# Four up blocks begun product by product in a hybrid RWKV-7 / attention decoder block, with two sums in a PSUM bank and attention heads scaled a tile later

## The chip, the cores and the metric

The kernel runs on one core of a Trainium2 chip. The metric is the device time of one execution in microseconds (us); lower is better. A run gives the time of each execution, and one profiled execution gives a trace of every instruction and DMA.

The engines are TensorE (PE, matmuls and transposes; PEld is its weight load), VectorE (DVE), ScalarE (ACT), GpSimd (POOL) and SyncE (SP). DMAs are issued from the queues of SP, ACT and POOL, and each queue issues in order: a DMA that must wait holds what stands behind it. PSUM has eight banks of 2 KB per partition, each 512 float32 columns.

## The reference

One decoder layer on 512 tokens, width 2048, float32: RWKV-7 time mixing and sliding-window attention in parallel, merged by sigmoid gates, then a gated FFN with a causal convolution of width 3 over the tokens.

```python
def reference(x, ...):
    h = rms_norm(x, norm1_g)
    z = h @ w_in                       # 2048 -> 9152 columns
    o_rw = rwkv7_mix(token_shift(z[:, :RW_SHIFT_COLS], rw_mu), ...)   # 16 heads of 64
    o_att = swa_attention(q, k, v, q_norm_g, k_norm_g, sinks)         # q and k: rms_norm by head of 64
    g_rw, g_att = sigmoid(zg[:, :2048]), sigmoid(zg[:, 2048:])
    x = x + (g_rw * (o_rw @ w_branch[:1024]) + g_att * (o_att @ w_branch[1024:])) @ w_out
    return x + conv_ffn(rms_norm(x, norm2_g), w_up, conv_w, conv_b, w_down)

def conv_ffn(h, w_up, conv_w, conv_b, w_down):
    u = h @ w_up                       # 2048 -> 2 * 5632
    c = conv_w[0] * u[t - 2] + conv_w[1] * u[t - 1] + conv_w[2] * u[t] + conv_b
    val, gate = split(c, 2)
    return (silu(gate) * val) @ w_down # 5632 -> 2048
```

## The kernel before, in words

Tokens are the free dimension of nearly all tiles (512 columns), features the partitions (128). Every large matmul is done in three: both factors are split into a high part (rounded to float32r by ACT, `whi`) and a low part (the rest, a subtraction on DVE, `wlo`), and hi x hi, hi x lo and lo x hi are summed in PSUM.

A planner orders the instructions of each engine by its own estimate of when they are ready; `pin` keeps an instruction behind all that was traced before it on its engine. Semaphores follow the data, and the tiles' buffers. All weight loads stand in SP's queue.

**Attention and RWKV (about 35 to 1230 us).** `ztile` computes one 128-column tile of z (48 matmuls, four weight loads of 256 KB through four `raw` buffers). A k or q tile goes through `qk_norm`: DVE multiplies by the gain (zq), ACT squares (sqq), PE sums by head (`head_stats`), DVE takes the inverse root in some 12 small instructions (rq), PE transposes it, DVE copies it (rsT), and `head_rows` writes it to DRAM (rsd) and reads it back spread over 64 partitions per head (rsb): three DMAs from ACT's queue, the last two waiting for the first to land. Then DVE multiplies z by rsb. The k tile is copied into kd by four more DMAs from ACT. `head_rows` also serves each of the eight RWKV pairs twice, in `early` and `final`. `sums_along` puts sums of quarters of w_out and w_down into DRAM at every third (later 16th) weight load.

**Branch products (about 1210 to 1445 us).** o_rw and o_att times w_branch, scaled by the gates, which are read back from DRAM (gin, two DMAs per tile from ACT).

**w_out and w_down** are each multiplied in seven half-size products (Winograd's form of Strassen's scheme) over halves of the tokens and of the columns; `taken_out` adds a finished product into x1 (L917). The last product of w_out reads x by then normalised by `normalise(0)` for its token half 0; `transposed` turns x1 into `q11` and `q21` (token half 0) and `q12` and `q22` (half 1), and `split_q` splits them into hi and lo.

**Up blocks (about 1628 to 2550 us).** 44 blocks f of 128 value and 128 gate columns of w_up, each with seven products P1, P2, P7, P6, P5, Q4, P3, of 24 matmuls of 256 columns, hi and lo parts made two products ahead (`prep(i + 2)`) through three buffers. P1 and P2 need only b11 and b21 (token half 0); P7, P5, P6 and Q4 need t3, t1, t2 and t4, and P3 needs b22: differences of all four quarters. Three PSUM sums: X takes P1, P6, P5, P3 one on top of the other and is read after each; Z takes P2; Y takes P7 and Q4. `out` brings them to u:

```python
            if n == "P7": return
            if n in ("P1", "P6"): ... act.activation(t, X, AF.Copy)        # t1, u2  (L1031)
            if n == "P2":   dve: u[:, 0, first half] = Z + t1               # L1035
            elif n == "P5": act: u4 = X; dve: u[:, 1, second half] = Y + u4 # L1038, L1039
            elif n == "Q4": dve: u[:, 1, first half] = Y + u2               # L1041
            else:           act: u[:, 0, second half] = X                   # P3, L1043
```

X and Z are each half a bank of a tile with two buffers of its own (four banks), Y has two. `conv` does the convolution in five to seven pieces, one per `prep`; `keep` stores the factors of a pair of blocks to DRAM, from ACT's queue, before the first piece of every second block. The order of the products is written out in `steps`; matmuls, splits and `out` are pinned. Two blocks are begun together; from block 2 the order is P7, P6, P2, P5, P1 of the next block, Q4, P3. Loads are issued in the order of `queue`, each group when a named earlier product has been prepared. a11 has two buffers; a12, s3, s1 and a22 share six; s3 and s1 are sums of two quarters, the second added by a DMA from POOL.

Of the kernel before, what the change touches and what calls it, by code (L numbers as in the profile page):

```python
# [134 lines left out]
def block_kernel(ctx: ExitStack, tc: tile.TileContext, d: Dims, a: dict, out: bass.AP):  # L135
# [147 lines left out]
    if True:  # L283
# [63 lines left out]

        with ExitStack() as pt:
# [7 lines left out]
            def qk_norm(acc, gain, dst):  # L356
                z = ap_.tile([P, S], F32, name="zq", tag="zq", bufs=2)
# [6 lines left out]
                rb = head_rows(ap_, small(), rs)  # L364
                dve.tensor_tensor(dst, z, rb, op=ALU.mult)
# [4 lines left out]
            for t in range(NKV):  # L370
                acc = ztile(d.c_ka + t * P)
                kn = ap_.tile([P, S], F32, name="kn", tag="kn", bufs=2)
                qk_norm(acc, col("kg"), kn)
                for h in range(2):
                    for e in range(2):
                        act.dma_start(kd[2 * t + h][e * HD : (e + 1) * HD], kn[h * HD : (h + 1) * HD])
                acc = ztile(d.c_va + t * P)
                vf = ap_.tile([P, S], F32, name="vf", tag="zq", bufs=2)
# [18 lines left out]
            for g in range(NHK):  # L397
# [3 lines left out]
                else:  # L401
                    emit_gate()
                oT = ap_.tile([P, GQ // 2, S], F32, name="oT", tag="oT", bufs=2)
# [358 lines left out]
        with tc.tile_pool(name="ain", bufs=1, side="right", reuse_waits="tile") as ainp:  # L762
# [24 lines left out]
    x1 = x1p.tile([P, NT, d.D], F32, name="x1")  # L787
# [29 lines left out]
    wp["step"] = 16  # L817
    with ExitStack() as pbb:
# [9 lines left out]
        for m, i in order:  # L828
            hi, lo, r0, n, gi = parts[i]
            second = m in g  # L830
            if not second:
                g[m] = tb.tile([P, 2, S], F32, name="gin", tag="gin")
                for j in range(2):
                    act.dma_start(g[m][:, j], gate_d[(j * NK + m) * P : (j * NK + m + 1) * P])
            acc = accp.tile([P, S], F32, name="acc", tag="acc")
            project(acc, a["w_b"][m].rearrange("p (k c) -> p k c", c=P)[:, r0 : r0 + n], hi, lo)
            if second:
                w = min(XC, d.D)
                for e in range(m * XC, (m + 1) * XC, w):
                    t, c0 = divmod(e, d.D)  # L840
                    with tc.issue_after(wp["last"].ins):
                        sync.dma_start(x1[:, t, c0 : c0 + w], xd[t * P : (t + 1) * P, c0 : c0 + w])
# [63 lines left out]
    def taken_out(i, acc, xr, scale, done):  # L906
        ci, tj, sign = PRODUCTS[i][4]
        last = i in (3, 4, 5, 6)
        for t in range(NT // 2):
            for e in range(NQW):  # L910
                tt = tj * NT // 2 + t
                cs = slice(ci * DH + e * S, ci * DH + (e + 1) * S)
                x = xr[:, tt, cs]
# [13 lines left out]
    q11, q12, q21, q22 = (x1[:, 2 * j : 2 * j + 2, i * WC : (i + 1) * WC] for i in range(2) for j in range(2))  # L927
    tpx = ExitStack()

    def row_done(i, t, cc, cs):  # L930
        sq = sqp.tile([P, S], F32, name="sqc", tag="sqc", bufs=2)
        act.activation(sq, x1[:, t, cs], AF.Square, accum_out=ssp[:, t, cc : cc + 1])
        (act if i == 6 else pool).dma_start(x1_d[t * P : (t + 1) * P, cs], x1[:, t, cs])

    def normalise(h):
# [3 lines left out]
        for i in range(2):  # L939
            for t in range(NT // 2):  # L940
                part = x1[:, 2 * h + t, i * WC : (i + 1) * WC]
# [5 lines left out]
    def transposed(tps, i, h, q):  # L947

        pss = []
        for k in range(KH):  # L950
            if k % 2 == 0:
                pss.append(tps.tile([P, 2, TH], F32, name="ps_t", tag="tp"))
            for t in range(NT // 2):
                pe.transpose(pss[-1][:, k % 2, t * P : (t + 1) * P],
                             x1[:, 2 * h + t, (i * KH + k) * P : (i * KH + k + 1) * P], ident)
# [19 lines left out]
    def half(nm, n=1):  # L975
        return up.tile([P, TH], F32, name=nm, tag=nm, bufs=n)

    class Block:
# [6 lines left out]
        def load(self, *names):  # L985
            f, w = self.f, self.w
            at = {"a11": (0, 0), "a12": (0, 1), "s3": (0, 0), "s1": (1, 0), "a22": (1, 1)}
            for n in names:
                w[n] = raw_tile("a11", 2) if n == "a11" else raw_tile()
                sync.dma_start(w[n], a["w_up"][(f, *at[n])])  # L990
            for n, i, j in (("s3", 1, 0), ("s1", 1, 1)):
                if n in names:
                    pool.dma_start(w[n], a["w_up"][f, i, j], accum_op=ALU.add)
# [8 lines left out]
        def parts(self, n):  # L1002
            t = self.w[{"P1": "a11", "P2": "a12", "P7": "s3", "P6": "a11", "P5": "s1", "Q4": "a22", "P3": "a11"}[n]]
# [5 lines left out]
        def mm(self, n):  # L1009
            if n == "P1":  # L1010
                self.X, self.Z = (ups.tile([P, S], F32, name=x, tag=x)[:, :TH] for x in "XZ")
# [3 lines left out]
            start = n in ("P1", "P2", "P7")  # L1015
# [8 lines left out]
        def out(self, n):  # L1024
# [3 lines left out]
            if n in ("P1", "P6"):  # L1028
                t = half("t1", 2) if n == "P1" else half("u2")
                setattr(self, "t1" if n == "P1" else "u2", t)  # L1030
                pin(act.activation(t, X, AF.Copy))  # L1031
                return
            u = us[self.f % 2]
            if n == "P2":
                pin(dve.tensor_tensor(u[:, 0, 2 : 2 + TH], Z, self.t1, op=ALU.add))  # L1035
            elif n == "P5":
                u4 = half("u4")
                pin(act.activation(u4, X, AF.Copy))  # L1038
                pin(dve.tensor_tensor(u[:, 1, 2 + TH :], Y, u4, op=ALU.add))  # L1039
            elif n == "Q4":  # L1040
                pin(dve.tensor_tensor(u[:, 1, 2 : 2 + TH], Y, self.u2, op=ALU.add))  # L1041
            else:
                pin(act.activation(u[:, 0, 2 + TH :], X, AF.Copy))  # L1043
# [31 lines left out]
    steps = [(0, "P1"), (1, "P1"), (0, "P2"), (1, "P2"), (0, "P7"), (1, "P7"), (0, "P6"), (0, "P5"), (0, "Q4"), (1, "P6")]  # L1075
    steps += [(0, "P3"), (1, "P5"), (2, "P1"), (1, "Q4"), (1, "P3")]
    for f in range(2, NF):
        steps += [(f, n) for n in (("P7", "P6", "P2", "P5") if f + 1 < NF else ("P7", "P6", "P5", "P2"))]
# [3 lines left out]
    queue = []  # L1082
    for f in range(NF):
        if f == 1:
# [214 lines left out]
```

## Time and profile before

| | |
|---|---|
| time, median of 3 runs | 2977.66 us (2977.48 to 2984.68) |
| profiled execution | 2978.18 us, span 2976.4 us |
| PE busy | 2890.1 us (97%), 18794 matmuls |
| DVE / ACT / POOL busy | 1949.3 / 1317.1 / 219.1 us |
| mean granted clock of PE | 0.988 |
| DMA | 605.26 MB, mean 203 GB/s |

A stage's row has its length, then the busy time (and number of instructions) of PE, PEld, DVE, ACT and POOL, the granted clock, the DMA share and GB/s. A row of the waits has the engine and what it would run, who released it, then us in total, times, longest. A row of a timeline has start, us, engine, line, operation, tiles and, in brackets, the idle time before it and its releaser; rows of the chain have start, us and what. Matmuls overlap, so one's recorded length is more than the time to the next. q after an engine's name means its queue.

### The profile page before, as it was taken

To read this page: it belongs to the slowest core of one execution; us is meant where nothing else is said; L and a number is where in the kernel's file an instruction comes from. 1 tells how busy PE (TensorE), PEld (TensorE's weight loads), DVE (VectorE), ACT (ScalarE), POOL (GpSimd) and SP (SyncE) were. 2 spreads that over 40 slices of the span, in tenths; PEclk is the share of its full clock that TensorE was granted. 3 is DMA by queue.
4 is the path that set the end of the run, shared out by engine and by line. 5 is a ranking of instruction groups with operands and counts; after the bars stand their busy time and mean duration, and the time that the engine had idled before them with its cause. 6 is when DMAs were issued, how large, how long until landed. Compare 5 with 4: busy or idle time off the path is not lost.

```text
span 2976.4 us, 48126 instructions
## 1 busy us (share of the span) xinstructions
PE 2890.1 (97%) x18794; PEld 2468.2 (83%) x18794; DVE 1949.3 (65%) x3243; ACT 1317.1 (44%) x2135; POOL 219.1 (7%) x286
## 2 busy tenths in 40 slices
PE   6899999999999999999999799999999999999999
PEld 5677877777777777678888799999999999888887
DVE  4365477676666666344567787777777778665555
ACT  4244344344344344232346545545554554544444
POOL 0000100000000000101000010111011010000000
PEclk9999999999999999999999899999999999999999
DMA  7744756657646657777877588888898887777775
GB/s 208 198 116 124 207 134 163 161 123 178 161 119 179 160 126 176 250 204 244 282 242 245 135 238 229 232 223 227 236 242 231 230 229 210 287 241 240 258 256 190
DMA packets 223989, 605.26 MB, mean 203 GB/s; under 512 B 24640, under 2 KB 44816, under 8 KB 222736
## 3 DMA queue, kind: packets, MB, share of 16 engines
q1 hardware_dynamic: 150624, 421.70, 44.1%
q0 software_dynamic: 36064, 132.14, 22.9%
q10 hardware_dynamic: 37072, 48.34, 4.8%
q8 instruction: 147, 2.41, 0.3%
q14 instruction: 82, 0.67, 0.1%
HBM read 552.43 MB, written 174.43 MB: 244 GB/s over the span
## 4 chain that ended last, share of the span: by engine, by line
PE 86%; DVE 4%; DMA 4%; ACT 2%; issue 1%; ACTq 0%; SPq 0%; DVEq 0%
PE X L1021 16%; PE X L903 11%; PE acc L259 9%; PE acc L260 9%; PE acc L258 9%; PE Y L1021 8%; PE Y L903 8%; PE Z L1021 4%; DMA rsb<-rsd 1%; DMA rsd<-rsT 1%; PE bulk L630 1%; PE bulk L692 1%; PE mi L446 1%; PE psG L699 1%; DMA raw<-in_w_z_dram 1%
## 5 line engine op out<-in xcount | busy, mean ns | idle before, releaser
L260 PE MATMUL acc<-xhi,wlo 128*128 128x512 f32 x1152 | 473.3, 411 | 3.1 <-DVE wlo L244 3.1
L258 PE MATMUL acc<-xhi,whi 128*128 128x512 f32 x1152 | 469.6, 408 | 6.0 <-ACT whi L243 4.1
L259 PE MATMUL acc<-xlo,whi 128*128 128x512 f32 x1152 | 470.1, 408 | 0.0
L243 ACT ACTIVATE whi<-raw 128x512 fp32r<-128x512 f32 x352 | 219.2, 629 | 478.1 <-PE acc L259 286.0
L244 DVE TENSOR_TENSOR wlo<-raw,whi 128x512 fp32r<-128x512 f32 x352 | 240.0, 688 | 247.3 <-ACT whi L243 243.1
L896 DVE TENSOR_TENSOR wlo<-raw,whi 128x1024 fp32r<-128x1024 f32 x210 | 257.1, 1225 | 207.0 <-ACT whi L895 205.4
L895 ACT ACTIVATE whi<-raw 128x1024 fp32r<-128x1024 f32 x210 | 222.5, 1060 | 288.6 <-PE X L903 151.2
L1021 PE MATMUL Y<-t,whi 128*128 128x256 f32 x1408 | 262.1, 286 | 16.9 <-ACT t L969 10.2
L1006 DVE TENSOR_TENSOR wlo<-raw,whi 128x1024 fp32r<-128x1024 f32 x176 | 215.1, 1222 | 77.7 <-ACT whi L1005 77.5
L1021 PE MATMUL X<-t,whi 128*128 128x256 f32 x1408 | 259.8, 285 | 4.9 <-ACT u L1031 4.9
L258 PEld LDWEIGHTS acc<-xhi,whi 128*128 128x128 f32 x1152 | 220.0, 191 | 48.4 <-ACT whi L243 5.4
L260 PEld LDWEIGHTS acc<-xhi,wlo 128*128 128x128 f32 x1152 | 219.9, 191 | 45.5 <-DVE wlo L244 5.1
L1021 PE MATMUL X<-b,whi 128*128 128x256 f32 x1408 | 257.2, 283 | 0.0
L259 PEld LDWEIGHTS acc<-xlo,whi 128*128 128x128 f32 x1152 | 219.9, 191 | 44.2 <-issue 2.9
L1021 PEld LDWEIGHTS Y<-t,whi 128*128 128x128 f32 x1408 | 223.4, 195 | 17.7 <-ACT t L969 10.4
L1005 ACT ACTIVATE whi<-a 128x1024 fp32r<-128x1024 f32 x132 | 139.3, 1056 | 217.9 <-DVE a L1000 217.6
L1021 PEld LDWEIGHTS X<-t,whi 128*128 128x128 f32 x1408 | 221.6, 194 | 5.3 <-ACT u L1031 5.3
L1021 PEld LDWEIGHTS X<-b,whi 128*128 128x128 f32 x1408 | 219.7, 192 | 0.1
L1006 DVE TENSOR_TENSOR wlo<-a,whi 128x1024 fp32r<-128x1024 f32 x132 | 161.8, 1225 | 72.2 <-ACT whi L1005 71.6
L1021 PE MATMUL Y<-t,wlo 128*128 128x256 f32 x704 | 201.3, 286 | 0.0
L1021 PE MATMUL X<-t,wlo 128*128 128x256 f32 x704 | 200.5, 285 | 0.1
L1021 PE MATMUL X<-b,wlo 128*128 128x256 f32 x704 | 199.2, 283 | 0.0
(337 smaller groups left out, 6057.9 us busy)
## 6 DMA issues: line engine op xcount, KB each, us to landing
raw<-in_w_up_dram SPq DMA_DIRECT2D x176, 512.0 KB
raw<-in_w_z_dram SPq DMA_DIRECT2D x288, 256.0 KB
s_dn<-in_w_dn_dram POOLq DMA_DIRECT2D x88, 512.0 KB, 6.4
raw<-in_w_up_dram POOLq DMA_DIRECT2D x88, 512.0 KB, 8.6
raw<-s_dn SPq DMA_DIRECT2D x88, 512.0 KB
raw<-in_w_dn_dram SPq DMA_DIRECT2D x66, 512.0 KB
s_dn<-in_w_dn_dram SPq DMA_DIRECT2D x44, 512.0 KB
s_dn<-s_dn SPq DMA_DIRECT2D x44, 512.0 KB
```

What stands on the lines that cost most here:

```text
L243: act.activation(hi, raw, AF.Copy)
L244: dve.tensor_tensor(lo, raw, hi.bitcast(F32), op=ALU.subtract)
L258: pe.matmul(acc, whi[:, j], xhi[:, k], start=first, stop=False)
L259: pe.matmul(acc, whi[:, j], xlo[:, k], start=False, stop=False)
L260: pe.matmul(acc, wlo[:, j], xhi[:, k], start=False, stop=last)
L446: pe.matmul(ps[:, h], pT[:, kb, h], vt[:, n - 1 + kb, g * HD : (g + 1) * HD], start=kb == kbs[0], stop=kb == kbs[-1])
L895: act.activation(whi, wr, AF.Copy)
L896: dve.tensor_tensor(wlo, wr, whi.bitcast(F32), op=ALU.subtract)
L903: pe.matmul(dst, l[:, q, ts], r[:, es], start=fst and j == 0, stop=lst and j == 2, skip_group_check=True)
L1005: pin(act.activation(hi, t, AF.Copy))
L1006: pin(dve.tensor_tensor(lo, t, hi.bitcast(F32), op=ALU.subtract))
L1021: pin(pe.matmul(ps, l[:, k], r[:, k], start=start and k + i == 0, stop=last and i == 2, skip_group_check=True))
```

## The change

- `head_rows` issues its three DMAs from SP in place of ACT, everywhere. In attention, the multiplication by rsb and the copies of k are left to the next `qk_norm` (`finish`), with three zq and two rsb buffers.
- Four blocks begin together (`NPRE`): P1 of blocks 0 to 3, then P2, then P7, then blocks 0 and 1, and 2 and 3, in pairs. a11 and a12 of these are loaded twice (p11, p12). Each load waits for the last reader of its buffer.
- X and Z of a block share one bank (`XZ`), four buffers; Y has four. P2 no longer starts a sum of its own.
- From block 4 P1 and P6 are copied to u at once by ACT, and P2, P5 and Q4 are added to u by DVE. In the last block P7 comes after P6. In the catch-up two conv pieces are done per step.
- x1 is four tiles, one for each quarter, so that its parts are freed apart. The transposes of q11 and q21 stand one chunk earlier in the last product of w_out.
- The gate loads of the first four tiles come from SP, pinned; `sums_along` runs at every fourth load in the last gates and every twelfth in the branch products.

```diff
-        def head_rows(pl, ps, rs, tag="lg"):
+        def head_rows(pl, ps, rs, tag="lg", bufs=1):
...
-            act.dma_start(rd, sm)
-            rb = pl.tile([P, S], F32, name="rsb", tag=tag)
+            sync.dma_start(rd, sm)
+            rb = pl.tile([P, S], F32, name="rsb", tag=tag, bufs=bufs)
...
-                act.dma_start(rb[h * HD : (h + 1) * HD], src[h : h + 1].to_broadcast([HD, S]))
+                sync.dma_start(rb[h * HD : (h + 1) * HD], src[h : h + 1].to_broadcast([HD, S]))
...
+            unscaled = []
+            def finish():
+                if unscaled:
+                    dst, z, rb, then = unscaled.pop()
+                    pin(dve.tensor_tensor(dst, z, rb, op=ALU.mult))
+                    then()
...
-                rb = head_rows(ap_, small(), rs)
-                dve.tensor_tensor(dst, z, rb, op=ALU.mult)
+                rb = head_rows(ap_, small(), rs, bufs=2)
+                finish()
+                unscaled.append((dst, z, rb, then))
...
+            wp["step"] = 4
...
-    wp["step"] = 16
+    wp["step"] = 12
...
+                    if m < 4:
+                        pin(sync.dma_start(g[m][:, j], src))
+                    else:
+                        act.dma_start(g[m][:, j], src)
...
         def mm(self, n):
             if n == "P1":
-                self.X, self.Z = (ups.tile([P, S], F32, name=x, tag=x)[:, :TH] for x in "XZ")
+                xz = ups.tile([P, S], F32, name="XZ", tag="XZ")
+                self.X, self.Z = xz[:, :TH], xz[:, TH:]
...
-            start = n in ("P1", "P2", "P7")
+            start = n in ("P1", "P7")
...
+            if n == "P1" and self.f < NPRE:
+                self.t1 = up.tile([P, TH], F32, name="t1", tag="t1", bufs=NPRE)
+                pin(act.activation(self.t1, X, AF.Copy))
                 return
...
+            i, j, ps, first = {"P1": (0, 0, X, True), "P2": (0, 0, Z, False), "P6": (1, 0, X, True), "P5": (1, 1, X, True),
+                               "Q4": (1, 0, Y, False), "P3": (0, 1, X, True)}[n]
+            u = us[self.f % 2][:, i, 2 + j * TH : 2 + (j + 1) * TH]
+            if first:
+                pin(act.activation(u, ps, AF.Copy))
+                if n == "P5":
+                    pin(dve.tensor_tensor(u, u, Y, op=ALU.add))
             else:
+                pin(dve.tensor_tensor(u, self.t1 if n == "P2" and self.f < NPRE else u, ps, op=ALU.add))
...
+    pre = range(NPRE)
+    steps = [(f, n) for n in ("P1", "P2", "P7") for f in pre]
+    for f in range(0, NPRE, 2):
+        steps += [(f + e, n) for e, n in ((0, "P6"), (0, "P5"), (1, "P6"), (0, "P3"), (1, "P5"), (0, "Q4"), (1, "P3"), (1, "Q4"))]
+    steps += [(NPRE, "P1")]
+    for f in range(NPRE, NF):
+        steps += [(f, n) for n in (("P7", "P6", "P2", "P5") if f + 1 < NF else ("P6", "P7", "P5", "P2"))]
         steps += [(f + 1, "P1")] if f + 1 < NF else []
         steps += [(f, "Q4"), (f, "P3")]
...
+    loads = [(f + e, n) for f in range(0, NPRE, 2) for n in ("p11", "p12") for e in range(2)] + [(f, "s3") for f in pre]
...
-                if last and c == NB["o"] - 3:
+                if last and c == NB["o"] - 4:
                     transposed(tps, 0, 0, q11)
...
-    ups = psx.enter_context(tc.tile_pool(name="upps", bufs=2, space=PSUM, reuse_waits="tile"))
+    ups = psx.enter_context(tc.tile_pool(name="upps", bufs=4, space=PSUM, reuse_waits="tile"))
...
+    run(10)
+    split_q("b22", q22)
+    run(11)
     dve.scalar_tensor_tensor(q21, q11, -1.0, q21, op0=ALU.mult, op1=ALU.subtract)
-    run(6)
     split_q("t4", q21)
...
     for f in range(2):
         B[f].out("P2")
-    for i in range(7, len(steps)):
+    for i in range(3 * NPRE, len(steps)):
         run(i)
+        if steps[i] in ((2, "P6"), (2, "Q4")):
+            B[2 + (steps[i][1] == "Q4")].out("P2")
```

More of the change, by code (lines that the diff above doesn't have):

```diff
@@ L372, in block_kernel, with copies @@
                 kn = ap_.tile([P, S], F32, name="kn", tag="kn", bufs=2)
[L373 to L376, printed above, removed]
+                def copies(t=t, kn=kn):
+                    for h in range(2):
+                        for e in range(2):
+                            act.dma_start(kd[2 * t + h][e * HD : (e + 1) * HD], kn[h * HD : (h + 1) * HD])
+                qk_norm(acc, col("kg"), kn, copies)
                 acc = ztile(d.c_va + t * P)
-                vf = ap_.tile([P, S], F32, name="vf", tag="zq", bufs=2)
+                vf = ap_.tile([P, S], F32, name="vf", tag="zq", bufs=3)
                 act.activation(vf, acc, AF.Copy)
@@ L786, in block_kernel, with x1 @@
     x1p = x1s.enter_context(tc.tile_pool(name="x1", bufs=1, side="right", reuse_waits="tile"))
-    x1 = x1p.tile([P, NT, d.D], F32, name="x1")
+    x1q = ExitStack()
+    x1r = x1q.enter_context(tc.tile_pool(name="x1r", bufs=1, side="right", reuse_waits="tile"))
+    xq = {(i, j): (x1r if (i, j) == (0, 1) else x1p).tile([P, NT // 2, DH], F32, name=f"x{i}{j}")
+          for i in range(2) for j in range(2)}
+    def x1(t, cs):
+        i, j = cs.start // DH, t // (NT // 2)
+        return xq[i, j][:, t % (NT // 2), cs.start - i * DH : cs.stop - i * DH]
     tcx = ExitStack()
@@ L1089, in block_kernel @@
+    held = {True: [], False: []}
+    for f, n in loads:
+        kind = n in ("p11", "a11")
+        users = {"p11": ("P1",), "p12": ("P2",), "s3": ("P7",), "s1": ("P5", "P6"), "a22": ("Q4",)}.get(n, ("P3",))
+        ring, deep = held[kind], 2 if kind else 6
+        queue.append((f, n, ring[-deep] if len(ring) >= deep else None))
+        ring.append(max(((f, u) for u in users), key=order.get))
     ready = set()
     def issue_loads():
-        while queue and (queue[0][2][0] < 0 or queue[0][2] in ready):
-            f, names, _ = queue.pop(0)
-            B[f].load(*names)
+        while queue and (queue[0][2] is None or queue[0][2] in ready):
+            f, n, _ = queue.pop(0)
+            B[f].load(n)
@@ L1096, in block_kernel, with some_later, prep @@
     later = []
-    def prep(i):
-        if i < len(steps):
-            f, n = steps[i]
-            B[f].sums(n)
+    def some_later(n):
+        for _ in range(n):
             if later:
                 later.pop(0)()
-            B[f].parts(n)
-            ready.add((f, n))
+    def prep(i, n=1):
+        if i < len(steps):
+            f, nm = steps[i]
+            B[f].sums(nm)
+            some_later(1)
+            B[f].parts(nm)
+            some_later(n - 1)
+            ready.add((f, nm))
```

105 lines of the change are left out of this document (44 added, 61 removed).

## The prediction

> **What bounds the kernel now.** I read the table of stages first (busy time of each engine in a stretch, then granted clock, DMA share, GB/s), then the waits of TensorE (PE), and then each stage's own rows. The first line is the page's head; stages without a line hold nothing for this change.
>
> ```profile
> span 2976.4 us, 48126 instructions
> ```
> ```profile
> 50.00:250.00 200.00, 180.05 (x902) 141.87 (x901) 94.96 (x316) 63.15 (x162) 13.78 (x17) 0.94 0.65 163
> ...
> 1200.00:1300.00 100.00, 92.55 (x414) 71.81 (x411) 35.84 (x73) 30.95 (x57) 13.03 (x19) 0.97 0.81 246
> ...
> 1628.00:1684.00 56.00, 36.20 (x251) 34.75 (x251) 46.07 (x53) 27.21 (x37) 3.94 (x7) 0.82 0.49 124
> 1684.00:2533.00 849.00, 848.92 (x7072) 848.57 (x7072) 665.48 (x798) 435.03 (x591) 87.20 (x101) 1.00 0.84 228
> 2533.00:2545.00 12.00, 8.02 (x45) 7.82 (x44) 7.04 (x9) 5.13 (x8) 0.00 (x0) 0.72 0.34 117
> ```
> ```profile
> PE mi L333 <- ACT sqq L360: 14.2, 5, 4.8
> PE Y L1021 <- ACT t L969: 10.2, 1, 10.2
> PE X L1021 <- ACT u L1031: 4.9, 2, 4.0
> PE Y L1021 <- DVE u L1039: 4.8, 1, 4.8
> PE mi L382 <- ACT vf L379: 4.4, 2, 2.8
> ```
>
> PE is the bound. In the 849 us of the steady up blocks it idles 849.00 - 848.92 = 0.08 us, at full clock: nothing can be won there, and every wait that is put between two products is paid in full. What can be won lies in four places: attention (50 to 250 us: 19.95 us idle, and a clock of 0.94), the start of the branch products (7.45 us idle), the change to the up blocks (1628 to 1684: 19.8 us idle, clock 0.82) and the last up block (3.98 us idle, clock 0.72).
>
> **The change, part 1: X and Z in one PSUM bank, in the steady blocks.** From block 4 on the order is P7, P6, P2, P5, P1 of the next block, Q4, P3, as before. P6 writes X, then ScalarE (ACT) copies X to u; P2 writes Z, then VectorE (DVE) adds Z; P5 writes X again. Before, Z had a bank of its own, so P2 covered the copy of X. Now both are halves of one tile. Does PE wait for a reader of the other half? No row shows a product against a reader at other columns; these show ACT against DVE:
>
> ```profile
> ACT sqq L360 <- DVE zq L358: 19.1, 10, 5.2
> ```
> ```profile
> 1641.15 1.55 ACT L962 ACTIVATE x<-ps_t,par 128x256 f32<-128x256 f32 x4
> ```
> ```profile
> 1641.66 0.02 DVEq L960
> ...
> 1642.02 0.02 DVEq L960
> ...
> 1642.39 0.02 DVEq L960
> ```
>
> sqq and zq both only read acc, yet one waits for the other, 10 times. In the third, DVE's evictions of the odd halves of ps_t are let go about 0.36 us apart, at the pace of ACT's evictions of the even halves in the same banks (1.55 us for 4). So accesses by two engines to one bank are ordered even where neither needs the other's data, and where the columns differ. I take it that a product and a reader are ordered too. The Trainium skill says so outright (PSUM — Partial Sum Buffer, "PSUM bank collisions raise a hardware error"): two engines in the same bank and 32-partition quadrant collide even at disjoint columns, TensorE's write against a read included, so a kernel must guard by bank. By that rule the sum below is 3019 us; by data dependences alone it would be 2942. The trace agrees for the two readers; for TensorE no row here shows it.
>
> So PE meets two new waits in each of the 39 blocks 4 to 42: P6 to P2 behind the copy, P2 to P5 behind the add. Their price, from the one place of before where PE waits for such a copy (P6 to P5 of block 0, both on X):
>
> ```profile
> 1669.30 0.28 PE L1021 MATMUL X<-t,wlo 128*128 128x256 f32 x1
> 1670.53 0.51 PE L1021 MATMUL X<-t,whi 128*128 128x256 f32 x2 [0.95 <-ACT u L1031]
> 1670.87 0.28 PE L1021 MATMUL X<-t,wlo 128*128 128x256 f32 x1
> ```
> ```profile
> 1670.11 0.37 ACT L1031 ACTIVATE u<-X 128x256 f32<-128x256 f32 x1
> ```
> ```profile
> 1986.68 2.88 PE X L1021 x24
> 1989.56 2.88 PE Z L1021 x24
> ```
> ```profile
> 2006.84 2.88 PE X L1021 x24
> 2009.72 2.88 PE Z L1021 x24
> ```
> ```profile
> 1989.60 0.38 ACT L1031 ACTIVATE u<-X 128x256 f32<-128x256 f32 x1
> ...
> 2010.75 0.37 ACT L1031 ACTIVATE u<-X 128x256 f32<-128x256 f32 x1
> ```
> ```profile
> 1992.81 0.42 DVE L1035 TENSOR_TENSOR u<-Z,t 128x256 f32<-128x256 f32 x1
> ...
> 2013.94 0.42 DVE L1035 TENSOR_TENSOR u<-Z,t 128x256 f32<-128x256 f32 x1
> ```
>
> A matmul takes 2.88 / 24 = 0.12, so the next was due at 1669.42; it came at 1670.53, 1.11 late, and the first two took 0.34 in place of 0.24: 1.21 lost. There the copy was late itself: the last matmul ended at 1669.58, the copy began at 1670.11. A prompt copy begins 0.04 after the end (1989.60 against 1989.56), so 0.49 less: 0.72 us. Behind an add of 0.42 it is 0.77. Even blocks: the copy is prompt as the rows stand, 0.72 + 0.77 = 1.49. Odd blocks: ACT has the DMAs of keep() in front, and the copy begins 1.03 after P6's end (2010.75 against 2009.72), 0.99 later than prompt: 1.71 + 0.77 = 2.48. For the adds I take the prompt price: as they stand they begin 0.37 and 1.34 after P2's end (1992.81 against 1992.44; 2013.94 against 2012.60), but P2 itself now begins 0.72 and 1.71 later, and DVE's list does not. Sum: 20 x 1.49 + 19 x 2.48 + 0.72 (P5 to P2 of the last block) = **+77.6**. Lower bound, all prompt: 39 x 1.49 + 0.72 = 58.8. Upper bound, adds as late as now: 20 x 0.33 + 19 x 1.30 more = 109.
>
> **Part 2: four blocks begin together.** DVE sets this stage (46.07 of 56 us busy). Before, PE had done nine products at 1684 and never idled after. Now out("P2") of block 0 is pinned behind the last split (t4), it reads Z of block 0, and P6 of block 0 writes the same bank: P6 cannot begin before DVE has worked off its whole list.
>
> ```profile
> 1668.17 1.22 DVE L1006 TENSOR_TENSOR wlo<-raw,whi 128x1024 fp32r<-128x1024 f32 x1
> 1669.31 2.28 DVE L970 TENSOR_TENSOR b<-x,b 128x2048 fp32r<-128x2048 f32 x1
> 1671.51 2.28 DVE L970 TENSOR_TENSOR t<-x,t 128x2048 fp32r<-128x2048 f32 x1
> 1673.83 0.76 DVE L1035 TENSOR_TENSOR u<-Z,t 128x256 f32<-128x256 f32 x2
> ```
> ```profile
> 2538.18 5.49 PE X L1021 x24
> ```
>
> DVE came to that add at 1673.83. Its list grows by four wlo at 1.14 (twelve in place of eight) and loses the split of b21 (2.20, now one chunk earlier, under the last product of w_out): +2.4, so P6 begins near 1676.6, with twelve products done; before, the twelfth was done at 1684 + 3 x 2.88 = 1692.6. That is 16 us. Given back: a product at the low clock after the idle (5.49 - 2.88 = 2.6), the wait P6 to P5 of block 0 (1.2) and of block 2, there with the add of its Z too (1.2 + 0.5), P3 of block 3 behind Q4's add and that of its Z (0.77 + 0.34), and 2 for DVE, which does two conv pieces per step there (a guess between 0 and 4): 8.6. So **-8**; range -16 (nothing given back) to +3 (the first transposes, one chunk earlier, also wait for normalise). Eight loads more (p11, p12: 4.2 MB) cost nothing: DMA is at 124 GB/s here against 246 in the branch stage, and POOL's four accumulating loads of s3 have eight products' time; without that cover they would cost 4.2 MB / 246 = 17 us.
>
> **Part 3: heads scaled a tile later.**
>
> ```profile
> 116.87 0.69 DVE L365 TENSOR_TENSOR qn<-zq,rsb 128x512 f32<-128x512 f32 x1 [4.32 <-DMA rsb<-rsd]
> ```
> ```profile
> 118.91 1.87 PE L333 MATMUL mi<-cst,sqq 128*128 128x2 f32 x8 [4.25 <-ACT sqq L360]
> ...
> 197.71 1.05 PE L333 MATMUL mi<-cst,sqq 128*128 128x2 f32 x8 [2.41 <-ACT sqq L360]
> ```
> ```profile
> 200.00:205.00 5.00, 5.00 (x20) 3.48 (x19) 4.45 (x26) 3.42 (x14) 0.00 (x0) 0.73 0.23 54
> ```
> ```profile
> 53.56 3.75 DMA rsd<-rsT
> 57.87 4.86 DMA rsb<-rsd
> ```
> ```profile
> SPq L240 <- DVE wlo L244: 85.7, 27, 6.9
> ```
>
> DVE waits in order for rsb, the next zq stands behind it, then sqq, then PE; ACT waits for the same rows ahead of vf. Both go: the multiplication comes a tile later (48 matmuls, 10.7 us at the branch stage's 92.55 us for 414), the DMAs leave ACT. At stake are the 20 us idle and some 8 of the 12 us that a clock of 0.94 takes from 200 (the rest falls into the idle). The clock falls even after 2.41 us of idle (0.73 in the next row). The Trainium skill (TensorE: Matmul & The Clock Gate, "What's actually happening") puts it after an idle window of about 3.4 us, so only the longest waits would count, 5 and not 8 us, and the sum would be some 2 us higher; the row decides. What is late next is rsb: it lands some 9 us after rsd's issue (53.56 to 62.73), just inside that tile, and the 78 DMAs of 26 head_rows now stand in SP's queue among the weight loads, where each pair of rsb waits until rsd has landed (3.75). Raw loads behind it are covered by four buffers at 2.7 us of PE each; SP mostly waits for these to come free (85.7 us in 27 waits). I take 7/10 of 28: **-20**, range -28 to -6.
>
> **Part 4: the rest.** Start of the branch products, gate loads for m < 4 from SP rather than ACT, and the paces 4 and 12 of the added sums: of 7.45 us idle, **-3** (-8 to +4, as the same loads can now stop SP). Last block: P7 moves between P6 and P5, which covers a copy: 3.98 idle and 2.6 of low clock before, **-5** (-6.6 to 0). x1 in four tiles, the rings by last reader, sixteen head_rows outside attention: nothing (PE idles 0.08 us in the blocks).
>
> **Sum.** The profiled execution took 2978.18 us (1.8 over its span, 0.5 over the median of 2977.66). 2978.2 + 77.6 - 8 - 20 - 3 - 5 = **3019.8**, say 3019.
>
> **The rivals.**
> - Bank sharing costs no wait (PE is held only by data): the gains alone, 2978 - 36 = 2942. For it: no row shows a product held by a reader of other columns. Against: two readers are held. It decides if the steady blocks still take 20.16 us. Chance 0.08.
> - Waits prompt, all gains full: 58.8 - 16 - 28 - 8 - 6.6 = 0, 2978. Against: keep() delays the copy by 1.03 now. Chance 0.08.
> - The adds stay as late as now (+31): 3050. Against: DVE's list is not held by P2. Chance 0.14.
> - SP's queue becomes the bound: each of 26 head_rows costs PE a weight tile's 2.7 us, and attention wins nothing: 3019 + 70 + 20 = 3109, less where the four buffers cover it. Chance 0.08.
>
> **How the numbers follow.** Forecast 0.62, with 2990 to 3048 as its own range. Slower by over 0.3% (9 us, about what a measurement of this kernel can tell from no change): 0.62 + 0.14 + 0.08 = 0.84; within: 0.08; faster: 0.08. The range 2978 to 3065 leaves out the first rival and the last.
>
> **What would show it.** Steady blocks of 21.6 and 22.6 us in turn; PE X and Z waiting for ACT u and DVE u, some 79 waits of 0.5 to 1.6 us; no drop of the clock there. Attention without waits of PE for sqq and vf, near 20 us shorter. P6 of block 0 waiting for DVE u. If the waits are there but the stages ahead won over 50 us, my part 3 is too small; if the blocks take 20.16, part 1 is wrong, and with it the sign.

## The result, and the profile after

The changed kernel takes 3027.14 us (median of 4 runs, 3023.94 to 3027.8), the kernel before 2977.57 beside it on the same chip: 1.0162 times as long, 95% interval 1.014 to 1.0184. It is slower, as forecast, and 8 us over the forecast of 3019. The profiled execution took 3026.59 us with a span of 3024.8, 48.4 more than the span of before.

The stages are best cut at instructions that both kernels have. Each row of these two timelines is a start in us, a length, the engine, the line, and the tiles: the last attention product, the first product of w_out, the first P1, P7 of block 4, the first product of w_down. First the kernel before, then the kernel after.

```profile
293.54 1.90 PE L446 MATMUL mi<-vt,pT 128*128 128x64 f32 x16
1467.99 0.40 PE L903 MATMUL X<-whi,hhi 128*128 128x512 f32 x1
1628.29 0.40 PE L1021 MATMUL X<-b,whi 128*128 128x256 f32 x2
1741.51 0.40 PE L1021 MATMUL Y<-t,whi 128*128 128x256 f32 x2
2552.44 0.39 PE L903 MATMUL X<-whi,hhi 128*128 128x512 f32 x1
```
```profile
265.58 1.90 PE L460 MATMUL mi<-vt,pT 128*128 128x64 f32 x16
1437.09 0.40 PE L931 MATMUL X<-whi,hhi 128*128 128x512 f32 x1
1598.56 0.48 PE L1049 MATMUL XZ<-b,whi 128*128 128x256 f32 x2 [0.88 <-DVE x L945]
1711.71 0.40 PE L1049 MATMUL Y<-t,whi 128*128 128x256 f32 x2
2598.80 0.40 PE L931 MATMUL X<-whi,hhi 128*128 128x512 f32 x1
```

Subtracting the starts (P7 of block 4 left out), and the last of them from the spans, gives the whole account:

| stage | before | after | difference | forecast |
|---|---|---|---|---|
| to the end of attention | 293.5 | 265.6 | -28.0 | -20 |
| RWKV and branch products | 1174.5 | 1171.5 | -2.9 | -3 |
| w_out | 160.3 | 161.5 | +1.2 | 0 |
| up blocks | 924.2 | 1000.2 | +76.1 | +77.6 - 8 - 5 = +64.6 |
| w_down | 424.0 | 426.0 | +2.0 | 0 |
| sum | 2976.4 | 3024.8 | +48.4 | +41.6 |

Inside the up blocks, the stretch from the first P1 to P7 of block 4, where the four blocks are begun, is 113.2 us before and 113.1 after: nothing was won there. All of the loss lies behind it. TensorE's waits in the steady blocks of the kernel after, by what it would run and who let it go (us in total, times, longest), and below them the busy time of its engines there (length, then PE, PEld, DVE, ACT, POOL, clock, DMA share, GB/s):

```profile
PE XZ L1049 <- ACT u L1065: 40.8, 40, 2.0
PE XZ L1049 <- DVE u L1069: 20.1, 39, 0.5
```
```profile
1714.00:2598.00 884.00, 823.11 (x6673) 807.00 (x6672) 640.17 (x760) 414.04 (x559) 83.02 (x96) 1.00 0.79 209
```

These are the 79 waits that the prediction counted: a copy and an add in each of 39 blocks, and one copy in the last. Semaphores that the program sets make these waits. In every run here two sums that share a bank are also halves of one tile, so no run can tell a wait by bank from a wait by tile. PE idles 884.00 - 823.11 = 60.9 us where it idled 0.08. The chain of waits of the kernel after shows one even block; below it are the first matmuls of P6 and of P2 in the timeline:

```profile
1983.83 2.89 PE XZ L1049 x24
...
1986.74 0.39 ACT u L1065
...
1987.18 3.14 PE XZ L1049 x24
...
1990.34 0.43 DVE u L1069
...
1990.82 3.16 PE XZ L1049 x24
```
```profile
1983.66 0.40 PE L1049 MATMUL XZ<-t,whi 128*128 128x256 f32 x2
...
1987.18 0.50 PE L1049 MATMUL XZ<-b,whi 128*128 128x256 f32 x2 [0.47 <-ACT u L1065]
```

P6, its copy, P2, its add, P5: one after the other, where the same boundaries had no gap before. From the end of P6 (1986.72) to P2 pass 0.46 us. And the chain counts 3.14 and 3.16 us for a product behind a wait, against 2.89. Most of that difference is the way of counting: a product that follows another is counted from the other's end, though its first matmul starts 0.17 us before it (1983.66 against 1983.83). Behind a wait this overlap is gone; what is longer in itself are the first two matmuls, 0.50 in place of 0.40. So a boundary costs 0.46 + 0.25 = 0.71 for a copy and 0.50 + 0.27 = 0.77 for an add (the prediction took 0.72 and 0.77). From block 5 on the blocks take 22.5 to 22.9 us (odd) and 21.65 (even) in turn, against 20.16; two odd blocks took 24.4.

In attention the waits of PE for sqq and vf are gone. PE's busy time of the kernel after there, at a clock of 1.00:

```profile
50.00:250.00 200.00, 199.08 (x1070) 157.19 (x1069) 111.07 (x360) 75.62 (x204) 15.38 (x19) 1.00 0.69 178
```

### The profile page after: what moved, and what is told of

It reads as the page before. It is cut to its first block, busy times and chain, and to the rows that moved or that the text cites. A ratio compares the mean times of both kernels' runs of the same rounds, so it can differ in the third digit from the quotient of the medians.

```text
span 3024.8 us, 48257 instructions
## 1 busy us (share of the span) xinstructions
PE 2910.5 (96%) x18794; PEld 2471.1 (82%) x18794; DVE 1959.6 (65%) x3243; ACT 1320.1 (44%) x2135; POOL 219.2 (7%) x286
## 3 DMA queue, kind: packets, MB, share of 16 engines
q8 instruction: 147, 2.41, 0.3%
## 5 line engine op out<-in xcount | busy, mean ns | idle before, releaser
L1049 PE MATMUL XZ<-b,whi 128*128 128x256 f32 x2112 | 392.8, 286 | 42.6 <-ACT u L1065 40.8
L1049 PEld LDWEIGHTS XZ<-b,whi 128*128 128x128 f32 x2112 | 331.0, 193 | 51.5 <-ACT u L1065 48.9
L923 ACT ACTIVATE whi<-raw 128x1024 fp32r<-128x1024 f32 x210 | 222.6, 1060 | 292.9 <-PE X L931 155.1
L1049 PE MATMUL XZ<-b,wlo 128*128 128x256 f32 x1056 | 300.1, 284 | 2.1 <-DVE wlo L1033 2.1
L1049 PE MATMUL XZ<-t,whi 128*128 128x256 f32 x1408 | 263.8, 288 | 31.0 <-DVE u L1069 30.5
L1049 PEld LDWEIGHTS XZ<-t,whi 128*128 128x128 f32 x1408 | 221.2, 194 | 39.6 <-DVE u L1069 33.8
L259 PEld LDWEIGHTS acc<-xlo,whi 128*128 128x128 f32 x1152 | 217.0, 188 | 41.6 <-issue 2.6
L1032 ACT ACTIVATE whi<-raw 128x1024 fp32r<-128x1024 f32 x176 | 184.3, 1048 | 64.9 <-PE XZ L1049 34.9
L1049 PEld LDWEIGHTS XZ<-b,wlo 128*128 128x128 f32 x1056 | 203.9, 193 | 2.3 <-DVE wlo L1033 2.3
```

The lines of the kernel that those rows point to most:

```text
L259: pe.matmul(acc, whi[:, j], xlo[:, k], start=False, stop=False)
L923: act.activation(whi, wr, AF.Copy)
L1032: pin(act.activation(hi, t, AF.Copy))
L1049: pin(pe.matmul(ps, l[:, k], r[:, k], start=start and k + i == 0, stop=last and i == 2, skip_group_check=True))
```

## Experiments

The theory: a product waits for a reader of another sum in its own PSUM bank (as the program's semaphores order it); this costs some 80 us, and the other parts give 30 back. The rivals: the new copies and adds, which write u itself, are the cost, or the lists of ACT and DVE.

### X and Z apart again, without more banks

Y's bank has a free half, and P7, which clears that bank, comes before P2 in every block from 4 on.

```diff
             if n == "P7":
-                self.Y = upy.tile([P, S], F32, name="Y", tag="Y")[:, :TH]
+                y = upy.tile([P, S], F32, name="Y", tag="Y")
+                self.Y = y[:, :TH]
+                if self.f >= NPRE:
+                    self.Z = y[:, TH:]
```

> From block 4 on Z takes the free half of Y's bank (P7, which clears that bank, comes before P2), so no product stands behind a reader of its own bank: P6 to P2 and P2 to P5 change the bank, and each copy and add has a whole product of 2.88 us beside it. Theory (bank order costs the time): the 39 + 39 waits of XZ for ACT u and DVE u go, the stretch from the last P7 of block 4 to w_down falls from 884.6 to some 808.5 us, and the time from 3027 to 2948 (2945 to 2955). Rival 1 (the waits come from the copies that now write u itself, or from ACT's and DVE's lists): the waits stay, 3027. Rival 2 (only the copies' half is the bank, the adds stay late): 39 x 0.7 us stay, some 2976.

Measured: 2947.59 us, ratio 0.9915 to before (0.99 to 0.9929). First P1 to w_down: 920.5 us. In the steady stretch of this kernel the two groups of waits are gone, and the chain of waits at the same place runs through P6, P2 (now in Y's bank), and P5 with P1 of the next block:

```profile
1714.00:2520.00 806.00, 802.72 (x6686) 802.14 (x6685) 635.17 (x763) 414.32 (x562) 82.83 (x96) 1.00 0.86 231
```
```profile
1978.64 2.88 PE XZ L1052 x24
1981.52 2.88 PE Y L1052 x24
1984.40 5.76 PE XZ L1052 x48
```

The same copies and adds, on the same lines into the same u, cost nothing once the product beside them is on another bank: as causes, both rivals fall. (ACT's list still sets how long a wait for a copy was, 0.47 us in the even blocks and 1.3 to 2.0 in the odd ones.) The wait comes back at one place, the last block, where P2 follows P5, whose add reads Y, the other half of Z's new bank, and Q4 follows P2:

```profile
2511.24 0.50 PE L1052 MATMUL Y<-b,whi 128*128 128x256 f32 x2 [2.20 <-DVE u L1070]
2515.21 0.47 PE L1052 MATMUL Y<-t,whi 128*128 128x256 f32 x2 [0.84 <-DVE u L1072]
```

There its six products take 20.8 us against 18.2 in the kernel after. In all, the edit takes 79.6 us off the changed kernel and leaves one that is faster than before.

### The kernel before, with X and Z in one bank

```diff
-                self.X, self.Z = (ups.tile([P, S], F32, name=x, tag=x)[:, :TH] for x in "XZ")
+                xz = ups.tile([P, S], F32, name="XZ", tag="XZ")
+                self.X, self.Z = xz[:, :TH], xz[:, TH:]
...
-            start = n in ("P1", "P2", "P7")
+            start = n in ("P1", "P7")
```

> The kernel before with one edit: X and Z are halves of one bank, everything else (order, temporaries, loads, attention) as it was. Theory (bank order): blocks 2 to 42 each pay P6 to P2 behind ACT's copy and P2 to P5 behind DVE's add, 21 even blocks x 1.49 + 20 odd x 2.48 + 0.72 in the last = 82 us by the prediction's prices: 3060 (3050 to 3070). Rival 1 (waits of the kernel after come from its other edits): 2978. Rival 2 (adds as late as in the kernel before, not moved by P2): some 33 us more, 3093.

Measured: 3059.43 us, ratio 1.0289 (1.0273 to 1.0304); first P1 to w_down 1002.6 us, 78.4 more than before. Its waits in the up blocks:

```profile
PE XZ L1022 <- ACT u L1032: 42.3, 42, 2.1
PE XZ L1022 <- DVE u L1036: 21.5, 41, 0.8
```

With this edit alone the loss is there, with the old temporaries, loads and order. The adds are not late either (at most 0.8 us), which settles the rival that gave 3050.

### The order P6, P7, P5, P2 in every block

```diff
-        steps += [(f, n) for n in (("P7", "P6", "P2", "P5") if f + 1 < NF else ("P6", "P7", "P5", "P2"))]
+        steps += [(f, n) for n in ("P6", "P7", "P5", "P2")]
```

> The kernel after, with the order of its last block in all blocks from 4 on: P6, P7, P5, P2. One bank still holds X and Z, but P7 stands between P6 and the next product on that bank, and P1 of the next block behind P2. Theory: only P5 to P2 waits (for ACT's copy): 39 x 0.72 = 28 us with prompt copies, 20 x 0.72 + 19 x 1.71 = 47 if the copy is late in odd blocks: 3027 - 76 + 28 to 47 = 2979 to 2998. Rival (not the bank but the new copies and adds themselves cost the time): 3027.

Measured: 2976.05 us, ratio 1.0005 (0.9996 to 1.0014). That is just under the 2979 to 2998 expected. One wait per block is left:

```profile
PE XZ L1049 <- ACT u L1065: 24.4, 40, 1.3
```

Of the 39 blocks 24 take 20.88 us, 0.72 over 20.16, and the mean is 21.03: in this order most copies are prompt. So the bank can stay shared where the order puts a product on another bank between a product and the next one on the same bank; each boundary left costs 0.72 where the copy is prompt.

### Heads as before; and the two halves of that edit

Three kernels after, with the head rows' DMAs back on ACT's queue, the multiplication back at once, or both.

```diff
-                finish()
-                unscaled.append((dst, z, rb, then))
+                dve.tensor_tensor(dst, z, rb, op=ALU.mult)     # "at once"
+                then()
...
-            sync.dma_start(rd, sm)
+            act.dma_start(rd, sm)                              # "ACT's queue", and rsb likewise
```

> The kernel after, with the head rows' three DMAs back on ACT's queue and the multiplication by rsb at once. Theory (these two make attention's gain): the last matmul mi<-vt,pT goes back from 267 to some 295 us after the start, and the time to 3027 + 28 = 3055 (3047 to 3060). Rival (the gain comes from the paces of the added sums and the other loads): attention stays at 267, time 3027.

> The kernel after with only the queue put back: the head rows' three DMAs stand in ACT's queue, the multiplication stays a tile later. Theory A (DVE's wait for rsb, in order ahead of the next zq, made attention's gain): attention ends near 267 as in the kernel after, and as RWKV ran 8 us shorter with the rows on ACT's queue (1163.5 against 1171.5 us in the run with heads as before), the time is some 3019. Theory B (ACT's DMAs that wait for rsd held sqq and vf): attention ends near 297, the time is some 3046.

> The kernel after with only the multiplication put back: at once, the DMAs in SP's queue. Theory A (the multiplication's wait on DVE made the loss): attention ends near 297 and RWKV keeps its 1171.5, some 3057. Theory B (ACT's queue did): attention ends near 267, some 3027. If both matter, attention ends between.

Measured:

| multiplication, queue | time | start of the last attention row | from there to RWKV's last product |
|---|---|---|---|
| later, SP (after) | 3027.14 | 265.6 | 923.6 |
| later, ACT | 3026.97 | 271.5 | 917.1 |
| at once, SP | 3042.59 | 284.9 | 924.7 |
| at once, ACT | 3048.2 | 298.4 | 917.3 |

(before: 293.5 and 916.3.) In attention the deferral is worth 19 us with the rows on SP and 27 with them on ACT, the queue 13 and 6. Executions of kernels with the same attention differ too, by up to 4.3 us (293.5 in the kernel before, 297.9 in the one with X and Z in one bank), so the 6 is near the noise. The deferral is the larger part, as theory A has it, and the queue matters at least where the multiplication is at once. PE's longest waits in the stretch from 50 us to the end of attention are, with both undone, with the multiplication at once on SP, and with it later on ACT:

```profile
PE mi L333 <- ACT sqq L369: 14.1, 5, 4.9
PE mi L395 <- ACT vf L392: 7.4, 2, 4.5
```
```profile
PE mi L333 <- ACT sqq L369: 6.9, 3, 3.8
PE scp L426 <- DVE sc L432: 2.9, 2, 2.7
```
```profile
PE mi L333 <- ACT sqq L369: 2.9, 2, 1.5
```

The last column of the table held a surprise: the RWKV pairs run 7 us longer when their head rows stand on SP's queue, which takes back all that SP's queue wins in attention once the multiplication is later. With everything undone the time rises by 21 us, not the 28 expected.

### Head rows by stage

On the kernel with Z in Y's bank: SP in attention, ACT for the 16 rows of RWKV.

```diff
+            eng = sync if bufs == 2 else act
-            sync.dma_start(rd, sm)
+            eng.dma_start(rd, sm)
```

> The kernel with Z in Y's bank, and the head rows' DMAs by stage: SP's queue in attention (with the multiplication a tile later), ACT's queue in the RWKV pairs as in the kernel before. Theory (on SP's queue the 16 head_rows of RWKV hold the weight loads behind them: 923.6 us from attention's end to RWKV's in the kernel after, 916.0 before, 917.1 with the rows on ACT's queue): RWKV falls by 7 to 8 us, the time from 2947.6 to some 2940. Rival (that difference is attention's end, which the other stage's work fills): 2946 to 2949.

Measured: 2941.63 us, ratio 0.988 (0.9862 to 0.9898); attention's last row at 265.7, RWKV 916.3 us. The 7 us are confirmed; of them 6 reach the time, as the stretch from the first P1 to w_down was 925.1 us in the profiled execution, 4.6 longer than with Z in Y's bank alone. The cause of the 7 us is not shown: PE has no wait for these rows on SP. In the 910 us from 270 on it was busy 906.08 us with 6346 matmuls in the kernel after, and 900.97 us with 6395 with the rows on ACT. PE's order differs between the two kernels, but no run isolates that.

### Where the gain of four blocks went

Five kernels with Z in Y's bank look at the transition. The stretch is that from the first P1 to w_down, 920.5 us before these edits (924.2 in the kernel before).

Z of blocks 0 to 3 added to t1 soon after P2, and t1 copied to u later:

```diff
+            if n == "P2" and self.f < NPRE:
+                pin(dve.tensor_tensor(self.t1, self.t1, Z, op=ALU.add))
+                return
...
-        B[f].out("P2")
+        B[f].place()          # act.activation(u, t1, Copy)
```

> The kernel with Z in Y's bank, and for blocks 0 to 3 Z is added to t1 in place two products after P2, and t1 is copied to u by ACT where the add stood. Theory (in the transition P6 of block 0 waits for the add behind DVE's list, and P5 of block 2 for its add behind conv pieces, 11 us of PE waiting for DVE u in 3 waits): these waits go, the stretch from the first P1 to w_down falls from 920.5 by 8 to 12 us, the time from 2948 to some 2938. Rival (DVE's work sets this stage, so another wait for DVE takes their place): 2946 to 2950.

Measured: 2946.03 us, stretch 921.8. The rival holds: P6 of block 0 began 47.6 us after the first P1 in place of 53.1, but the wait for the add became one for the copy of P6, 8.7 us in 2 waits, 5.7 the longest.

The s3 loads of blocks 0 to 3 traced behind normalise(1):

```diff
-        while queue and (queue[0][2] is None or queue[0][2] in ready):
+        while queue and (queue[0][2] is None or queue[0][2] in ready) and (queue[0][1] != "s3" or sent):
...
     normalise(1)
+    sent.append(1)
```

> The kernel with Z in Y's bank, and the four s3 loads (with POOL's accumulating halves) of blocks 0 to 3 are issued only after normalise(1) is traced, behind the stores of x1. Theory (normalise(1) was late, ACT idle 9.4 us, because these loads crowded the x1_d stores that must read x before it is overwritten): ACT's wait for the stores falls from 9.4 to some 4 us, and the time by 3 to 6 us to some 2943. Rival (the stores take as long without the loads, or DVE sets the stage anyway): 2948; if P7 of block 0 then waits for s3, slower by up to 6 us.

Measured: 2948.72 us, stretch 920.1. It tells nothing of its theory: SP's queue holds the same loads in the same order as without the edit, and each goes as soon as its buffer is free, whatever was traced before it; ACT's wait for the stores stayed at 8.2 us. It is a repeat, and agrees within 1.1 us.

Two blocks begun in place of four, the four splits then made one after the other:

```diff
-    NPRE = 4
+    NPRE = 2
```

> The kernel with Z in Y's bank, and NPRE 2 in place of 4: two blocks begin together with six products, then t1, t2, b22 and t4 are split as fast as DVE can. Theory (the twelve products cover DVE's list, as the prediction had it, and something else gave the gain back): the stretch from the first P1 to w_down grows from 920.5 by 8 to 16 us, the time to 2956 to 2964. Rival (the list and the waits behind it set the end in both, the four blocks win nothing): 920 to 923, 2946 to 2950.

Measured: 2952.39 us (2947.2 to 2954.89), stretch 922.2 in the profiled execution, which was the shortest. By its time it is some 5 us worse than four, between theory and rival; its stretch, 1.7 us longer, fits the rival.

P1 and P2 of blocks 0 and 1 first, and the last stores of x1 in SP's queue ahead of the loads for blocks 2 and 3:

```diff
-    steps = [(f, n) for n in ("P1", "P2", "P7") for f in pre]
+    steps = [(f + e, n) for f in range(0, NPRE, 2) for n in ("P1", "P2") for e in range(2)] + [(f, "P7") for f in pre]
...
-        (act if i == 6 else pool).dma_start(x1_d[...], x1(t, cs))
+        pin(sync.dma_start(...)) if i == 6 else pool.dma_start(...)
```

> The kernel with Z in Y's bank; blocks 0 and 1 have P1 and P2 first (whose loads are there by then), then blocks 2 and 3; the four last x1_d stores stand in SP's queue, pinned ahead of the loads p11 of block 2 and all that follow, in place of ACT's queue beside them. Theory (normalise(1) is late because 1 MB of stores shares the DMA engines with these loads): ACT's wait for the stores falls from 8.4 to some 4 us as in the kernel before (2.6), all that hangs on normalise(1) comes 4 us sooner, 2944. Rival (stores take as long, or DVE's list sets the end anyway): 2946 to 2950, or slower by the 4 us that p11 of block 2 now comes later.

Measured: 2948.97 us, stretch 920.4. Here the cause was right and the gain nil. ACT's half of normalise(1), in the kernel after and in this one:

```profile
1611.92 2.19 ACT L971 ACTIVATE x<-x,rq 128x1024 f32<-128x1024 f32 x2 [9.35 <-DMA x_d<-x]
```
```profile
1607.46 2.20 ACT L971 ACTIVATE x<-x,rq 128x1024 f32<-128x1024 f32 x2 [2.54 <-DMA x_d<-x]
```

It came 6.2 us after the first P1 in place of 13.4, P6 of block 0 began 49.7 us after it in place of 53.8, and the end did not move, because a wait for DVE at P6 to P5 grew, to 7.9 us from 6.0 with Z in Y's bank alone and 5.5 in the kernel after. That place, P6 to P5 of block 2, in the kernel after, on PE, ACT and DVE:

```profile
1685.96 0.80 PE L1049 MATMUL XZ<-t,whi 128*128 128x256 f32 x2 [5.51 <-DVE u L1069]
```
```profile
1682.60 1.06 ACT L1032 ACTIVATE whi<-a 128x1024 fp32r<-128x1024 f32 x1 [3.50 <-DVE a L1026]
1683.56 0.80 ACT L1083 ACTIVATE c<-u,par 128x512 f32<-128x512 f32 x1
1684.27 0.36 ACT L1065 ACTIVATE u<-XZ 128x256 f32<-128x256 f32 x1
```
```profile
1681.27 1.22 DVE L1026 TENSOR_TENSOR a<-a,raw 128x1024 f32<-128x1024 f32 x1
...
1684.83 0.75 DVE L1086 SCALAR_TENSOR_TENSOR c<-u,par,c 128x512 f32<-128x512 f32 x1
1685.49 0.41 DVE L1069 TENSOR_TENSOR u<-t,XZ 128x256 f32<-128x256 f32 x1
```

P6 had ended near 1680.4. Its copy stands on ACT behind the high part of the product after next, which waits for a sum on DVE; the add of Z stands on DVE behind that sum and a piece of the convolution. P5 needs both done, since X and Z of block 2 share a bank.

So the last kernel has all of this (the early add, the stores first, the rows by stage), copies P6 of blocks 0 and 2 before those parts are made, and loads s1 of blocks 2 and 3 ahead of a11 and a12:

```diff
+        first = n == "P6" and f in (0, 2)
+        if not first:
             prep(i + 2, ...)
         B[f].mm(n)
         ... B[f].out(n)
+        if first:
+            prep(i + 2, 2)
...
+            loads += [(2, "s1"), (2, "a11"), (3, "s1"), (2, "a12"), (2, "a22"), (3, "a11"), (3, "a12"), (3, "a22")]
```

> Z in Y's bank, the head rows by stage, Z added to t1 early, the stores of x1 ahead of the loads of blocks 2 and 3, and two edits more in the transition: P6 of blocks 0 and 2 is copied to u before the parts of the product after next are made (in the kernel after, that copy stood behind ACT's whi, which waited for a sum on DVE, and P5 of block 2 waited 5.5 us), and s1 of blocks 2 and 3 is loaded ahead of a11 and of a12. Theory (P6 to P5 of block 2, 7 us of delay and 3 of low clock, is where the gain of four blocks went): the stretch from the first P1 to w_down falls from 920.5 to 910 to 915 us, the time to 2930 to 2936. Rival (the next wait on DVE's list takes its place, as in the two attempts before): 920, 2939 to 2942.

Measured: 2931.87 us (2931.05 to 2932.58), ratio 0.9852 (0.9835 to 0.987), stretch 912.1. The largest of PE's waits left from the first P1 on, to 1705 us:

```profile
PE XZ L1055 <- DVE wlo L1036: 4.8, 6, 1.9
PE XZ L1055 <- ACT u L1074: 3.8, 4, 2.1
PE XZ L1055 <- ACT t L1067: 2.8, 1, 2.8
```

It is the fastest: 44 us under the kernel before, 95 under the changed one. From the first P1 to P7 of block 4 it takes 101.5 us in place of 113.2, and 2.4 of that come back in block 4 (22.6 us). So a gain of the size forecast for the transition is there once the waits at P6 go; which of these edits makes it, alone or together, was not taken apart.

## Why the prediction was right, and where its sizes were off

- **Bank sharing (+77.6): right.** From the start of P7 of block 4 to the start of the last block it cost 82.2 us, and 0.8 in the last block. The copy was prompt in even blocks and late in odd ones, the adds were prompt, as the prediction chose. Of the 5 us over, 3.5 are two odd blocks of 24.4 us at a lower clock (below), which I had excluded. The rule of the Trainium skill that it weighed (PSUM — Partial Sum Buffer, "PSUM bank collisions raise a hardware error": guard by bank, also at disjoint columns) gave the right time. The trace agrees that product and reader of one bank, here always one tile, are kept apart, by semaphores that the program sets; what the chip would do without them no run shows.
- **Transition (-8): failed, within its range; it gave 0.** (Its own terms, 16 less 8.6, give 7.4.) Two of these terms fell. "P6 begins near 1676.6" is 48.3 us after the first P1; it began 53.8 after, with the same twelve products done:

```profile
1652.31 0.77 PE L1049 MATMUL XZ<-t,whi 128*128 128x256 f32 x2 [4.96 <-DVE u L1069]
```
```profile
1636.90 2.19 ACT L943 ACTIVATE x<-x,rq 128x1024 f32<-128x1024 f32 x2 [2.64 <-DMA x_d<-x]
```

  I moved DVE's list only by the work on it, and took eight more loads for free on DMA. But the list hangs on normalise(1) (the second row is ACT's half of it before), which may not overwrite x until the x1_d stores have read it, and these came beside the new loads: it came 13.4 us after the first P1 against 8.6 before, 4.8 of the 5.4 us that P6 was late. Then I gave back 1.7 us at P6 to P5 of block 2, and 7.2 were lost there, to work that stands ahead of the evictions on ACT and DVE, and to the low clock behind it. In return P6 and P5 of block 0 lost 2.1 in place of 3.8, and the 2 for DVE's conv pieces did not show. So 16 less 5.4 less 10.5 is 0.
- **Heads (-20): right mechanism, too small.** It won 28.0, the full upper end, of which some 4 can be the scatter named above. I took 7/10 of the stake because rsb lands just inside a tile. It does land inside: PE has no wait behind it, and DVE one, of 2.6 us.
- **Branch start and the rest (-3): right sum, wrong parts.** The branch stage won 10.3 us (258.2 to 247.9 from RWKV's last product to w_out), and RWKV lost 7.3, by the head rows on SP that I had put at nothing. Which of the edits to the branch stage won there no run shows.
- **Last block (-5): right.** Its six products took 18.2 us in place of 24.2: -6.0 with the one copy in it.
- w_out and w_down lost 1.2 and 2.0; the latter is as long as a new wait of PE, w_down's X for the last block's copy of XZ (one, 2.1 us), which I had not looked for.

That the sum came within 8 us is in part luck: the heads won 8 us more than forecast, and the transition 8 less.

The rival of the adds that stay late (3050) is ruled out by the 0.5 us of their longest wait, the one without bank waits (2942) by the 79 waits, the one of prompt waits (2978) by the copies that are late in odd blocks, and the one of SP's queue (3109) by the 28 us that attention won. With the bank cost taken away the time came to 2947.6, against 2975.1 for the kernel before beside it: the gains of the other parts together are some 28 us, against 36 forecast.

## What to carry to other kernels

Count the PSUM banks, not the sums: in this program two sums in one bank turn every eviction of the one into a wait before the next product on the other, some 0.7 us each where the eviction is prompt, unless a product on another bank stands between; a free half of another bank gave nearly all of it back, another order some 60%. When a stage is set by the list of an engine, look at what each piece on it waits for before counting only its work; and move an eviction ahead of the work made in advance on the same engine. A DMA that leaves one queue for another can win in one stage and lose in the next (here 7 us, by a way that stays open): move it stage by stage.

## What the runs showed of the hardware that was not expected

- The 79 waits, most of them near 0.5 us, left the mean clock at 1.00 over 884 us, but after two longer ones, of 1.75 and 2.02 us, it fell. After the one of 1.75 us the product took 4.6 us in place of 3.14, and the granted clock of the 20 us around it (the number after POOL's) was 0.91:

```profile
2187.43 0.62 PE L1049 MATMUL XZ<-b,whi 128*128 128x256 f32 x2 [1.75 <-ACT u L1065]
2192.58 0.51 PE L1049 MATMUL XZ<-t,whi 128*128 128x256 f32 x2 [0.52 <-DVE u L1069]
```
```profile
2180.00:2200.00 20.00, 17.74 (x133) 17.33 (x132) 12.47 (x14) 9.31 (x14) 1.72 (x2) 0.91 0.85 233
```

The Trainium skill (TensorE: Matmul & The Clock Gate, "What's actually happening") has the clock fall after an idle window of about 3.4 us. The trace does not agree: here it fell after single idles of 1.75 and 2.02 us, and in attention before after 2.41. Waits of 1.33 to 1.72 us in the 17 other odd blocks from block 5 on did not slow the product behind them (3.13 to 3.14 us).
